# Gate and up projections of a SwiGLU block: more K-pairs in the seven-product form

## The chip, the core and the metric

The kernel runs on one core of a Trainium2 chip. TensorE (PE) multiplies, VectorE (DVE) and ScalarE (ACT) prepare operands and read results, SyncE (SP) issues the weight loads, GpSimd (POOL) has a little work at the start. The metric is the device time of one execution in microseconds (us), shown as the median of three runs. Besides these runs there is one profiled execution; its rows are what is read below.

## The reference, cut to what matters

One decoder layer on 256 tokens of width 2048: a mixer (not touched here), and then the SwiGLU block, followed by a final norm:

```
def swiglu(h, w_gate, w_up, w_down):
    return (jax.nn.silu(h @ w_gate) * (h @ w_up)) @ w_down

h = h + swiglu(rms_norm(h, norm_ffn[l]), w_gate[l], w_up[l], w_down[l])
```

`w_gate` and `w_up` are 2048 x 5632, `w_down` is 5632 x 2048, all float32. Every product is made from float32 operands that are cut into a high part (rounded to the multiplier's format) and a low part (the rest), as three matmuls: high x high, low x high, high x low.

## The kernel before

**Chunks and parts.** The 5632 hidden columns are cut into 11 chunks of 512 (`f` = 0 to 10). For a chunk the 512 gate columns and the 512 up columns are computed together. `PARTS` (L34) groups the chunks: 0 to 2, 3 to 5, 6 to 8, 9 to 10. After the chunks of a part come the products with their rows of `w_down` ("down"), four groups of 512 output columns. In a part of three the words first, middle and last chunk are used below.

**Pairs, units, forms.** The 2048 rows of a chunk's weights are 16 K-tiles, taken as eight pairs p = 0 to 7. A pair is a product of 2x2 blocks: two token tiles by two K-tiles, and two K-tiles by gate and up. In the eight-product form (kind "N") a pair is one unit of 8 block products, 24 matmuls of 512 columns. In the seven-product form (kind "W", Winograd's) it is two units: "Wp" with 3 block products (9 matmuls) and "Ws" with 4 (12 matmuls). Below, N3, P4 and S4 mean the N unit of pair 3 and the Wp and Ws units of pair 4; with a prime (N0', P2') they belong to the next chunk. `FFN_KINDS` (L35) gives the kinds of the eight pairs, the same for all chunks: units N0 N1 P2 S2 N3 P4 S4 N5 P6 S6 N7. The table `PRODUCTS` (L390) names for each product the PSUM bank it is added to: seven banks, numbered 1 to 7, hold a chunk's sums. There are eight banks in all (L63).

**Cutting a unit's weights (L422 to L437).** For an N unit ACT writes the high parts of the 4 blocks (L108, 128x2048) and DVE subtracts for the low parts (L109, 128x2048). For a Wp unit DVE first makes four sums of weight blocks (L433 to L435), then ACT and DVE cut 3 blocks (128x1536). The Ws unit cuts the four sums (128x2048); ACT can start only after L435.

**The tokens' side.** `Halves` keeps the tokens' high and low parts; `differences` (L150 to L169) adds what a pair's form needs: two difference blocks for N, four for W, high and low, in tiles of 16 blocks from the pool `late`, which holds three. With five N and three W pairs the 44 blocks fill three tiles. `fill` (L177) makes one pair from a transposed PSUM bank: two ACT copies, a split, then `differences`.

**Ends of a chunk.** After the last Ws unit of a chunk `squares_early` (L459, L460) reads three of the seven banks; after the last unit `squares_end` (L467 to L471) reads the other four. Then ACT applies SiLU (L944), DVE multiplies (L947, twice), and PE transposes the result in two halves (L954, four transposes each; called T0 and T1 here), each into a bank of its own, which is split into high and low by ACT and DVE (L956). This is a side chain of steps, of which one is taken after a unit: `squares_end` and SiLU after the first unit of the following chunk, the L947 after the second, T0 after the third, T1 after the fourth (for the last chunk of a part each one unit earlier).

**What sets the order.** The program is written out in order; each engine takes its instructions in that order and waits for semaphores. `run` (L486 to L547) decides it: before unit j is multiplied, units ahead of it are cut, up to four, as long as the `need` of the units from j on (2 for N, 3 for Wp, 2 for Ws) is at most `cap` = 9. Then unit j is multiplied, then at most one side step is taken. Weights, cuts, sums and activations share the pool `slots` of 22 buffers (L61); a new tile waits until the last reader of the buffer's former tile is done.

Of the kernel before, what the change touches and what calls it, by code (L numbers as in the profile page):

```python
# [11 lines left out]
F32R = mybir.dt.float32r  # L12
# [4 lines left out]
P = 128  # L17
# [14 lines left out]
KT = D_MODEL // P  # L32
CH = 512
PARTS = ((0, 3), (3, 6), (6, 9), (9, 11))  # L34
FFN_KINDS = "NNWNWNWN"  # L35
GATE_KINDS = "NWNWNWWN"


# [13 lines left out]
def trunk(ctx: ExitStack, tc: tile.TileContext, x, norm_mix, norm_ffn, w_in, w_pool, pool_scale,  # L52
# [19 lines left out]
    def name(s):  # L72
        uid[0] += 1
        return f"{s}_{uid[0]}"

    def slot(shape, dt=F32):
        return slots.tile([P] + shape, dt, tag="slot", name=name("slot"))

    def late_slot(shape, dt=F32):
        return late[0].tile([P] + shape, dt, tag="late", name=name("late"))  # L80
# [6 lines left out]
    def wk(dt=F32):  # L87
        return work.tile([P, CH], dt, tag="wk", name=name("wk"), bufs=8)
# [4 lines left out]
    def bank():  # L93
        return psum.tile([P, CH], F32, tag="bank", name=name("bank"))
# [4 lines left out]
    def cols(n):  # L99
        return slice(n * CH, (n + 1) * CH)  # L100

    def toks(t):
        return slice(t * P, (t + 1) * P)

    def split(hi, lo, src, scale=None):

        if scale is None:
            nc.scalar.activation(hi, src, AF.Copy)  # L108
            nc.vector.tensor_tensor(lo, src, f32(hi), OP.subtract)  # L109
        else:  # L110
            nc.scalar.activation(hi, src, AF.Copy, scale=scale)
            nc.vector.scalar_tensor_tensor(lo, src, scale, f32(hi), OP.mult, OP.subtract)
# [4 lines left out]
    class Lazily(dict):  # L117


        def __init__(self, make):  # L120
            self.make = make
# [5 lines left out]
    class Halves:  # L127
# [10 lines left out]
        def pair(self, p):  # L138

            part, k = self.parts[p // 2], p % 2 * 2  # L140
            return part[:, k:k + 2, 0, :], part[:, k:k + 2, 1, :]

        def slab(self, p, s):

            if isinstance(s, tuple):
                return [o[:, toks(s[1])] for o in self(2 * p + s[0])]
            tile, at, n = self.ext[p]
            return tile[:, at + s, :], tile[:, at + n + s, :]

        def differences(self, p, a):  # L150

            e = wk().rearrange("p (n s) -> p n s", s=P)
            n = 4 if self.kinds[p] == "W" else 2
            if n == 2:
                nc.vector.tensor_tensor(e[:, 0:2], a[:, :, 0], a[:, :, 1], OP.subtract)
            else:
                f = a.rearrange("p k t s -> p (k t) s")
                nc.vector.tensor_tensor(e[:, 0:2], f[:, 1:2].to_broadcast([P, 2, P]), f[:, 0:4:3], OP.subtract)
                nc.vector.tensor_tensor(e[:, 2], f[:, 0], e[:, 1], OP.subtract)
                nc.vector.tensor_tensor(e[:, 3], f[:, 2], e[:, 2], OP.subtract)  # L160
            for i, (tile, used) in enumerate(self.tiles):
                if used + 2 * n <= 16:
                    break
            else:
                i, tile, used = len(self.tiles), late_slot([16, P], F32R), 0
                self.tiles.append(None)
            self.tiles[i] = tile, used + 2 * n
            self.ext[p] = tile, used, n
            split(tile[:, used:used + n], tile[:, used + n:used + 2 * n], e[:, 0:n])  # L169

        def add_differences(self, p):
# [93 lines left out]
    def beside(gen, after=2, lag=2):  # L265
        side.append([clock[0] + after, lag, gen])
# [129 lines left out]
    class Squares:  # L396


        def __init__(self, lhs, load, after, early, before=None, kinds=FFN_KINDS):
            self.lhs, self.load, self.after, self.early, self.before = lhs, load, after, early, before  # L400
# [8 lines left out]
    class Square:  # L409
# [29 lines left out]
        def multiply(self):  # L439
            g = self.g  # L440
            wh, wl = self.w
            del self.w
            todo = PRODUCTS[self.kind]
            slab = [(b, *g.lhs().slab(self.p, s), k) for b, s, k in todo]
            steps = [(b, x, wh, k) for b, xh, xl, k in slab for x in (xh, xl)] + [(b, xh, wl, k) for b, xh, _, k in slab]
            for b, x, w, k in steps:
                start = b not in g.banks
                if start:
                    g.banks[b] = bank()
                g.left[b] -= 1  # L450
                nc.tensor.matmul(g.banks[b], x, w[:, k, :], start=start, stop=g.left[b] == 0)  # L451
            if self.ends:
                g.early(g.banks)

    def squares_early(b):

        c12, w, x = wk(), wk(), wk()
        nc.scalar.activation(c12, b[1], AF.Copy)
        nc.vector.tensor_tensor(w, b[6], c12, OP.subtract)  # L459
        nc.vector.tensor_tensor(x, b[7], w, OP.add)  # L460
        return c12, w, x
# [331 lines left out]
    mT, h, hT = [], [], []  # L793
# [131 lines left out]
    def load_gf():  # L925
        gf.append(slot([D_MODEL]))
        nc.sync.dma_start(gf[0], bass.AP(tensor=norm_final.tensor, offset=norm_final.offset,
                                         ap=[[0, P], [1, D_MODEL]]))

    def swiglu(f, last):  # L930

        early = []

        def load(raw, p):
            for i, w in enumerate((w_gate, w_up)):
                nc.sync.dma_start(raw[:, :, i, :], w[2 * p * P:2 * (p + 1) * P, cols(f)].rearrange("(j p) c -> p j c", p=P))

        def begin(b):
            early.append(squares_early(b))

        def finish(b):
            c = squares_end(b, early[0])
            for t in range(NT):
                nc.scalar.activation(c[t][0], c[t][0], AF.Silu, scale=rstd2[t])  # L944
            yield
            for t in range(NT):
                nc.vector.scalar_tensor_tensor(c[t][1], c[t][1], rstd2[t], c[t][0], OP.mult, OP.mult)  # L947
            yield
            act[f] = a = slot([8, SEQ], F32R)
            for k in range(2):  # L950
                pt = bank()
                for i in range(2):
                    for t in range(NT):
                        nc.tensor.transpose(pt[:, i * SEQ + t * P:i * SEQ + (t + 1) * P],  # L954
                                            c[t][1][:, (2 * k + i) * P:(2 * k + i + 1) * P], ident)
                split(a[:, 2 * k:2 * k + 2, :], a[:, 4 + 2 * k:6 + 2 * k, :], pair(pt))  # L956
                if k == 0:
                    yield
            ready.add(f)

        def before():
            cap[0] = 9

        def after(b):
            beside(finish(b), after=1 if last else 2, lag=1)

        return Squares(lambda: hT[0], load, after, begin, before)

    def down(part, n):
        f0, f1 = PARTS[part]  # L970
# [62 lines left out]
    for part, (f0, f1) in enumerate(PARTS):  # L1033
        for f in range(f0, f1):
            groups += [swiglu(f, f == f1 - 1)]
        k = 2 if f1 - f0 > 2 else 3
# [43 lines left out]
```

## Time and profile before

| | |
|---|---|
| time, median of 3 runs (lowest to highest) | 1556.91 us (1556.3 to 1557.02) |
| profiled execution, its own time | 1557.08 us |
| its span from first to last instruction | 1555.3 us |
| PE busy | 1543.5 us (99%) |
| DVE busy | 1093.0 us (70%) |
| ACT busy | 745.4 us (48%) |
| DMA | 192 GB/s over the span, queue q1 at 56.1% of 16 engines |

The span is 1.8 us shorter than the profiled execution's time; the rest lies around the span. Matmul ends are modelled, so the spacing of matmuls is better read from the chain of waits, where a piece has a start, a length and a count. A timeline row whose count is above 1 has merged instructions that follow each other; the bracket at its end is the idle time before it and what ended that.

### The profile page before, as it was taken

The page shows a single profiled execution, that of the slowest core. Times are in us where ns is not written, and L with a number is a line of the kernel's source. Part 1 is how long each engine was busy: PE and PEld are TensorE (multiplying, and loading weights), DVE is VectorE, ACT ScalarE, POOL GpSimd, SP SyncE. Part 2 cuts the span into 40 slices and gives each one's busy share as a digit, 9 for nine tenths or more (in the row PEclk, how much of TensorE's full clock was granted, in tenths as well). Part 3 has the DMA queues.
Part 4 walks back from the last instruction along what each step waited for, and adds up shares of the span by engine and source line. Part 5 has one row for each costly group of instructions (what it writes and reads, how often), then busy time and mean ns, then how long its engine had stood idle before and what let it go on. Part 6 is the DMA issues. An engine that isn't in the chain of part 4 may idle for free.

```text
span 1555.3 us, 19158 instructions
## 1 busy us (share of the span) xinstructions
PE 1543.5 (99%) x7895; PEld 1322.2 (85%) x7895; DVE 1093.0 (70%) x1056; ACT 745.4 (48%) x718; POOL 25.8 (2%) x94
## 2 busy tenths in 40 slices
PE   9999999999999999999999999999999999999997
PEld 9998999988888888888888788888888888888886
DVE  6453655644568898978656988666985769857685
ACT  7323343446555545546455555434554435544353
POOL 2000000101100000000000000000000000000000
PEclk9999999999999999999999999999999999999999
DMA  9654455554555746647554566555575555655651
GB/s 349 221 189 163 138 186 170 165 186 160 169 171 186 259 137 242 236 143 270 196 201 151 189 211 220 188 187 184 195 239 187 169 190 191 241 189 167 213 217 55
DMA packets 144456, 300.13 MB, mean 193 GB/s; under 512 B 6464, under 2 KB 8048, under 8 KB 144240
## 3 DMA queue, kind: packets, MB, share of 16 engines
q1 hardware_dynamic: 143600, 297.44, 56.1%
q8 instruction: 62, 1.02, 0.3%
q0 software_dynamic: 304, 1.06, 0.2%
q10 hardware_dynamic: 464, 0.40, 0.1%
q14 instruction: 26, 0.21, 0.0%
HBM read 296.77 MB, written 2.11 MB: 192 GB/s over the span
## 4 chain that ended last, share of the span: by engine, by line
PE 97%; DVE 1%; ACT 0%; issue 0%; DMA 0%; ACTq 0%; DVEq 0%
PE bank L451 38%; PE bank L344 14%; PE bank L345 14%; PE bank L349 14%; PE bank L364 5%; PE bank L372 5%; PE bank L366 5%; DVE slot L109 1%; PE bank L954 1%; PE bank L596 0%; DMA slot<-in_x_dram 0%; ACT slot L108 0%; PE bank L597 0%; PE bank L851 0%; PE bank L907 0%
## 5 line engine op out<-in xcount | busy, mean ns | idle before, releaser
L109 DVE TENSOR_TENSOR slot<-slot,slot 128x2048 fp32r<-128x2048 f32 (+3 forms) x406 | 718.9, 1798 | 185.5 <-ACT slot L108 184.9
L108 ACT ACTIVATE slot<-slot 128x2048 fp32r<-128x2048 f32 (+3 forms) x406 | 600.8, 1516 | 340.2 <-DVE slot L435 136.0
L451 PE MATMUL bank<-slot,slot 128*128 128x512 f32 x1719 | 439.2, 390 | 0.0
L451 PEld LDWEIGHTS bank<-slot,slot 128*128 128x128 f32 x1719 | 321.8, 188 | 66.5
L344 PE MATMUL bank<-slot,slot 128*128 128x512 f32 (+1 forms) x936 | 364.3, 390 | 0.0
L345 PE MATMUL bank<-slot,slot 128*128 128x512 f32 (+1 forms) x936 | 362.3, 388 | 0.0
L451 PE MATMUL bank<-slot,late 128*128 128x512 f32 x1014 | 279.3, 390 | 0.0
L349 PE MATMUL bank<-slot,slot 128*128 128x512 f32 (+1 forms) x936 | 236.5, 387 | 0.0
L451 PEld LDWEIGHTS bank<-slot,late 128*128 128x128 f32 x1014 | 189.7, 188 | 39.1
L344 PEld LDWEIGHTS bank<-slot,slot 128*128 128x128 f32 x936 | 175.9, 188 | 35.2
L345 PEld LDWEIGHTS bank<-slot,slot 128*128 128x128 f32 x936 | 175.9, 188 | 35.2
L349 PEld LDWEIGHTS bank<-slot,slot 128*128 128x128 f32 x936 | 174.9, 188 | 35.9
L364 PE MATMUL bank<-slot,slot 128*128 128x256 f32 x640 | 158.6, 286 | 0.0
L366 PE MATMUL bank<-slot,slot 128*128 128x256 f32 x640 | 156.9, 283 | 0.0
L366 PEld LDWEIGHTS bank<-slot,slot 128*128 128x128 f32 x640 | 122.8, 192 | 0.0
L364 PEld LDWEIGHTS bank<-slot,slot 128*128 128x128 f32 x640 | 122.7, 192 | 0.1
L372 PE MATMUL bank<-slot,slot 128*128 128x256 f32 x640 | 89.8, 283 | 0.0
L372 PEld LDWEIGHTS bank<-slot,slot 128*128 128x128 f32 x640 | 82.6, 192 | 0.0
L108 ACT ACTIVATE slot<-bank 128x512 fp32r<-128x512 f32 x38 | 22.6, 594 | 123.5 <-PE bank L954 67.8
L109 DVE TENSOR_TENSOR slot<-bank,slot 128x512 fp32r<-128x512 f32 x38 | 26.2, 689 | 54.0 <-ACT slot L108 54.0
L433 DVE TENSOR_TENSOR slot<-slot 128x1024 f32<-128x1024 f32 x49 | 59.6, 1217 | 0.0
L989 DVE TENSOR_TENSOR slot<-bank,slot 128x512 f32<-128x512 f32 x30 | 19.6, 685 | 55.5 <-PE bank L349 55.5
(162 smaller groups left out, 631.3 us busy)
## 6 DMA issues: line engine op xcount, KB each, us to landing
slot<-in_w_in_dram SPq DMA_DIRECT2D x103, 1024.0 KB, 5.0
slot<-in_w_gate_dram SPq DMA_DIRECT2D x88, 512.0 KB, 3.9
slot<-in_w_up_dram SPq DMA_DIRECT2D x88, 512.0 KB, 4.8
slot<-in_w_down_dram SPq DMA_DIRECT2D x44, 1024.0 KB, 5.1
slot<-in_w_out_dram SPq DMA_DIRECT2D x16, 1024.0 KB, 5.2
slot<-in_w_br_a_dram SPq DMA_DIRECT2D x8, 1024.0 KB, 5.0
slot<-in_w_br_b_dram SPq DMA_DIRECT2D x8, 1024.0 KB, 5.1
slot<-in_w_br_c_dram SPq DMA_DIRECT2D x8, 1024.0 KB, 5.0
```

Of the source, the lines that this page charges most:

```text
L108: nc.scalar.activation(hi, src, AF.Copy)
L109: nc.vector.tensor_tensor(lo, src, f32(hi), OP.subtract)
L344: nc.tensor.matmul(acc[:, c], hi[:, toks(t)], whi[:, j, c], start=i + j == 0, stop=False)
L345: nc.tensor.matmul(acc[:, c], lo[:, toks(t)], whi[:, j, c], start=False, stop=False)
L349: nc.tensor.matmul(acc[:, c], hi[:, toks(t)], wlo[:, j, c], start=False, stop=i + j == n - 1)
L364: nc.tensor.matmul(o, whi[:, j, w], hi, start=i + j == 0 and c % 2 == 0, stop=False, skip_group_check=True)
L366: nc.tensor.matmul(o, whi[:, j, w], lo, start=False, stop=False, skip_group_check=True)
L372: nc.tensor.matmul(o, wlo[:, j, w], hi, start=False, stop=i + j == n - 1 and c % 2 == 1, skip_group_check=True)
L433: nc.vector.tensor_tensor(s[:, 0:2], raw[:, 0:1].to_broadcast([P, 2, CH]), raw[:, 1:3], OP.add)
L451: nc.tensor.matmul(g.banks[b], x, w[:, k, :], start=start, stop=g.left[b] == 0)
L954: nc.tensor.transpose(pt[:, i * SEQ + t * P:i * SEQ + (t + 1) * P], c[t][1][:, (2 * k + i) * P:(2 * k + i + 1) * P], ident)
L989: nc.vector.tensor_add(h[t][:, cs], acc[t], h[t][:, cs])
```

## The change

`FFN_KINDS` gets a third letter, "B" at pair 1: both forms are prepared for it on the tokens' side, and each chunk picks one. The chunks in `inner` (1, 4 and 7, the middle chunks of the parts of three) take N as before; the other eight chunks take W, and their units are N0 P1 S1 P2 S2 N3 P4 S4 N5 P6 S6 N7. `slab`, `ext` and `differences` get the kind as a second key. The tokens' differences need 52 blocks instead of 44; where a fourth tile is opened, it comes from `slots` instead of `late`.

```
-FFN_KINDS = "NNWNWNWN"
+FFN_KINDS = "NBWNWNWN"
...
-        def slab(self, p, s):
+        def slab(self, p, kind, s):
...
-            tile, at, n = self.ext[p]
+            tile, at, n = self.ext[p, kind]
...
         def differences(self, p, a):
 
+            for kind in "WN" if self.kinds[p] == "B" else self.kinds[p]:
+                self.differences_of(kind, p, a)
+
+        def differences_of(self, kind, p, a):
             e = wk().rearrange("p (n s) -> p n s", s=P)
-            n = 4 if self.kinds[p] == "W" else 2
+            n = 4 if kind == "W" else 2
...
-                i, tile, used = len(self.tiles), late_slot([16, P], F32R), 0
+                i = len(self.tiles)
+                tile, used = (late_slot if i < 3 else slot)([16, P], F32R), 0
...
-            slab = [(b, *g.lhs().slab(self.p, s), k) for b, s, k in todo]
+            slab = [(b, *g.lhs().slab(self.p, self.kind[0], s), k) for b, s, k in todo]
...
+    inner = [f for f0, f1 in PARTS for f in range(f0 + 1, f1 - 1)]
...
-        return Squares(lambda: hT[0], load, after, begin, before)
+        return Squares(lambda: hT[0], load, after, begin, before, FFN_KINDS.replace("B", "N" if f in inner else "W"))
```

The built program has 2709 matmuls of the line L451 (L456 in the changed kernel) where there were 2733.

**VectorE at the start of a last chunk.** Before, at the start of chunk 5, from the first instruction of chunk 4's `squares_end`:

```order
L467 TENSOR_TENSOR wk_1104_8714<-bank_1067_8467,wk_1104_8714 128x512
L468 TENSOR_TENSOR wk_1116_8786<-bank_1067_8467,wk_1105_8715 128x512
L469 TENSOR_TENSOR wk_1104_8714<-bank_1068_8472,wk_1104_8714 128x512
L470 TENSOR_TENSOR wk_1103_8713<-bank_1065_8457,wk_1103_8713 128x512
L471 TENSOR_TENSOR wk_1105_8715<-bank_1066_8462,wk_1105_8715 128x512
L109 TENSOR_TENSOR slot_1118_8795<-slot_1099_8682,slot_1117_8794 128x2048
L947 SCALAR_TENSOR_TENSOR wk_1103_8713<-wk_1103_8713,st2_6_103,wk_1104_8714 128x512
L947 SCALAR_TENSOR_TENSOR wk_1105_8715<-wk_1105_8715,st2_6_103,wk_1116_8786 128x512
L109 TENSOR_TENSOR slot_1121_8837<-bank_1122_8838,slot_1121_8837 128x512
L433 TENSOR_TENSOR slot_1125_8847<-slot_1102_8698 128x1024
L434 TENSOR_TENSOR slot_1125_8847<-slot_1125_8847,slot_1102_8698 128x512
L435 TENSOR_TENSOR slot_1125_8847<-slot_1125_8847,slot_1102_8698 128x512
```

After the change the same place, from the fourth instruction of `squares_end` (L475 and L476 are L470 and L471 of before, L438 to L440 are L433 to L435, L954 is L947):

```order
L475 TENSOR_TENSOR wk_1114_8736<-bank_1076_8479,wk_1114_8736 128x512
L476 TENSOR_TENSOR wk_1116_8738<-bank_1077_8484,wk_1116_8738 128x512
L438 TENSOR_TENSOR slot_1127_8811<-slot_1107_8673 128x1024
L439 TENSOR_TENSOR slot_1127_8811<-slot_1127_8811,slot_1107_8673 128x512
L440 TENSOR_TENSOR slot_1127_8811<-slot_1127_8811,slot_1107_8673 128x512
L109 TENSOR_TENSOR slot_1126_8810<-slot_1107_8673,slot_1125_8809 128x1536
L954 SCALAR_TENSOR_TENSOR wk_1114_8736<-wk_1114_8736,st2_6_103,wk_1115_8737 128x512
L954 SCALAR_TENSOR_TENSOR wk_1116_8738<-wk_1116_8738,st2_6_103,wk_1124_8801 128x512
L109 TENSOR_TENSOR slot_1130_8830<-slot_1127_8811,slot_1129_8829 128x2048
L109 TENSOR_TENSOR slot_1133_8837<-slot_1110_8704,slot_1132_8836 128x2048
L109 TENSOR_TENSOR slot_1137_8857<-bank_1138_8858,slot_1137_8857 128x512
L109 TENSOR_TENSOR slot_1137_8857<-bank_1139_8874,slot_1137_8857 128x512
```

Before, N3 was cut ahead of the two multiplications, and the low part of the first transposed half (the 128x512 row that reads a bank) followed them at once. Now the cut of P2 stands ahead of them, and the cuts of S2 and N3 stand between them and that low part.

**TensorE at T1 of the same chunk.** Before:

```order
L451 MATMUL bank_1129_8862<-slot_1110_8752,late_763_6437 128x512
L451 MATMUL bank_1130_8865<-slot_1110_8752,late_763_6437 128x512
L451 MATMUL bank_1113_8763<-slot_1110_8752,slot_784_6564 128x512
L954 MATMUL bank_1131_8874<-ident_84,wk_1103_8713 128x128 [waits DVE_49]
L954 MATMUL bank_1131_8874<-ident_84,wk_1105_8715 128x128
L954 MATMUL bank_1131_8874<-ident_84,wk_1103_8713 128x128
L954 MATMUL bank_1131_8874<-ident_84,wk_1105_8715 128x128
L451 MATMUL bank_1112_8758<-slot_1117_8794,slot_784_6564 128x512 [waits Activation_49]
```

After the change (L961 is L954 of before):

```order
L456 MATMUL bank_1128_8817<-slot_1126_8810,slot_785_6570 128x512
L456 MATMUL bank_1120_8773<-slot_1126_8810,slot_785_6570 128x512
L456 MATMUL bank_1123_8788<-slot_1126_8810,late_787_6577 128x512
L961 MATMUL bank_1139_8874<-ident_84,wk_1114_8736 128x128 [waits DVE_49]
L961 MATMUL bank_1139_8874<-ident_84,wk_1116_8738 128x128
L961 MATMUL bank_1139_8874<-ident_84,wk_1114_8736 128x128
L961 MATMUL bank_1139_8874<-ident_84,wk_1116_8738 128x128
L456 MATMUL bank_1122_8783<-slot_1129_8829,late_787_6577 128x512 [waits Activation_49]
```

In both programs T1 takes the bank that T0 had, since the other seven hold the chunk's sums, and so it waits for the DVE instruction that reads T0's bank last. Before, T0 stood after P2 (57 matmuls into the chunk) and T1 after S2; now T0 stands after S1 (45 matmuls) and T1 after P2.

**VectorE at the start of the first chunk.** Before, from the low part of S2 in chunk 0 (128x2x256 rows are the splits of pairs 6 and 7 of the tokens, `late` rows their differences):

```order
L109 TENSOR_TENSOR slot_827_6855<-slot_823_6818,slot_826_6854 128x2048
L109 TENSOR_TENSOR slot_835_6897<-wk_834_6894,slot_835_6897 128x2x256
L158 TENSOR_TENSOR wk_836_6900<-wk_834_6894 128x256
L159 TENSOR_TENSOR wk_836_6900<-wk_834_6894,wk_836_6900 128x128
L160 TENSOR_TENSOR wk_836_6900<-wk_834_6894,wk_836_6900 128x128
L109 TENSOR_TENSOR late_837_6904<-wk_836_6900,late_837_6904 128x512
L109 TENSOR_TENSOR slot_839_6908<-slot_814_6744,slot_838_6907 128x2048
L109 TENSOR_TENSOR slot_835_6897<-wk_842_6943,slot_835_6897 128x2x256
L155 TENSOR_TENSOR wk_843_6948<-wk_842_6943 128x256
L109 TENSOR_TENSOR late_837_6904<-wk_843_6948,late_837_6904 128x256
```

After the change, from the differences of pair 6 on (its split stands ahead of these rows, right behind the two L918, which are L913 of before):

```order
L163 TENSOR_TENSOR wk_835_6900<-wk_833_6894,wk_835_6900 128x128
L164 TENSOR_TENSOR wk_835_6900<-wk_833_6894,wk_835_6900 128x128
L109 TENSOR_TENSOR late_813_6744<-wk_835_6900,late_813_6744 128x512
L438 TENSOR_TENSOR slot_838_6908<-slot_804_6696 128x1024
L439 TENSOR_TENSOR slot_838_6908<-slot_838_6908,slot_804_6696 128x512
L440 TENSOR_TENSOR slot_838_6908<-slot_838_6908,slot_804_6696 128x512
L109 TENSOR_TENSOR slot_837_6907<-slot_804_6696,slot_836_6906 128x1536
L109 TENSOR_TENSOR slot_834_6897<-wk_841_6929,slot_834_6897 128x2x256
L159 TENSOR_TENSOR wk_842_6934<-wk_841_6929 128x256
L109 TENSOR_TENSOR slot_843_6936<-wk_842_6934,slot_843_6936 128x256
L109 TENSOR_TENSOR slot_845_6940<-slot_838_6908,slot_844_6939 128x2048
L109 TENSOR_TENSOR slot_848_6947<-slot_816_6751,slot_847_6946 128x2048
```

P1 and S1 are now cut where N1 and P2 were, ahead of L913; P2 and S2, of which only S2 was left and stood ahead of pair 6, are cut behind it.

## Rows read from the trace of the kernel before

**Rows 1.** The page: span, two engines' busy time, and the shares of the chain of work that ended last.

```profile
span 1555.3 us, 19158 instructions
PE 1543.5 (99%) x7895; PEld 1322.2 (85%) x7895; DVE 1093.0 (70%) x1056; ACT 745.4 (48%) x718; POOL 25.8 (2%) x94
...
PE 97%; DVE 1%; ACT 0%; issue 0%; DMA 0%; ACTq 0%; DVEq 0%
```

**Rows 2.** The chain of waits in order of time (start, length, engine, tile, line, count), at the first chunk of all and in the part of chunks 3 to 5.

```profile
849.12 12.29 PE bank L451 x54
861.44 2.28 DVE slot L109
...
892.80 1.33 DVE wk L947 x2
894.73 2.76 PE bank L451 x12
...
1032.49 54.40 PE bank L451 x240
1087.33 2.76 PE bank L451 x12
1090.52 38.80 PE bank L451 x171
1129.76 2.78 PE bank L451 x12
```

**Rows 3.** Busy time of the engines in four stretches: the output projection ahead of chunk 0; the three chunks 3 to 5; around T0 of chunk 0's result; the end of the program. Columns: stretch, its length, busy us and (in brackets) instructions of PE, PEld, DVE, ACT and POOL, granted clock, DMA share, GB/s.

```profile
725.00:837.00 112.00, 112.00 (x515) 92.67 (x514) 71.52 (x69) 55.87 (x64) 0.00 (x0) 1.00 0.61 205
...
1032.50:1160.00 127.50, 127.50 (x571) 105.56 (x571) 107.44 (x86) 60.41 (x42) 0.00 (x0) 1.00 0.60 202
...
892.00:898.00 6.00, 4.82 (x25) 3.58 (x25) 4.64 (x6) 1.97 (x2) 0.00 (x0) 1.00 0.58 181
...
1550.00:1555.30 5.30, 0.00 (x0) 0.00 (x0) 0.00 (x0) 0.05 (x1) 0.00 (x0) 0.53 0.60 198
```

**Rows 4.** The timeline of DVE from the end of chunk 4's cuts to the first transposed half of its result (chunk 5 begins inside).

```profile
1103.04 8.90 DVE L109 TENSOR_TENSOR slot<-slot,slot 128x2048 fp32r<-128x2048 f32 x4 [0.38 <-ACT slot L108]
1111.86 0.68 DVE L459 TENSOR_TENSOR wk<-bank,wk 128x512 f32<-128x512 f32 x1
...
1113.18 1.22 DVE L433 TENSOR_TENSOR slot<-slot 128x1024 f32<-128x1024 f32 x1
...
1115.77 1.75 DVE L109 TENSOR_TENSOR slot<-slot,slot 128x1536 fp32r<-128x1536 f32 x1
1117.90 2.29 DVE L109 TENSOR_TENSOR slot<-slot,slot 128x2048 fp32r<-128x2048 f32 x1 [0.38 <-ACT slot L108]
1120.11 0.68 DVE L467 TENSOR_TENSOR wk<-bank,wk 128x512 f32<-128x512 f32 x1
...
1122.50 0.68 DVE L471 TENSOR_TENSOR wk<-bank,wk 128x512 f32<-128x512 f32 x1
1125.19 2.29 DVE L109 TENSOR_TENSOR slot<-slot,slot 128x2048 fp32r<-128x2048 f32 x1 [2.02 <-ACT slot L108]
1127.40 1.41 DVE L947 SCALAR_TENSOR_TENSOR wk<-wk,st,wk 128x512 f32<-128x512 f32 x2
1130.42 0.69 DVE L109 TENSOR_TENSOR slot<-bank,slot 128x512 fp32r<-128x512 f32 x1 [1.61 <-ACT slot L108]
```

**Rows 5.** The timeline of DVE in chunk 3: its start, its last cut, the early reading of its banks, and the low part of its first transposed half.

```profile
1032.30 1.29 DVE L989 TENSOR_TENSOR slot<-bank,slot 128x512 f32<-128x512 f32 x2 [6.19 <-PE bank L349]
...
1059.46 2.29 DVE L109 TENSOR_TENSOR slot<-slot,slot 128x2048 fp32r<-128x2048 f32 x1 [0.25 <-ACT slot L108]
1068.41 0.69 DVE L459 TENSOR_TENSOR wk<-bank,wk 128x512 f32<-128x512 f32 x1 [6.66 <-PE bank L451]
...
1088.06 0.69 DVE L109 TENSOR_TENSOR slot<-bank,slot 128x512 fp32r<-128x512 f32 x1 [2.74 <-ACT slot L108]
```

**Rows 6.** The timeline of DVE in chunk 0, from L913 to the two L947.

```profile
838.28 1.28 DVE L913 TENSOR_TENSOR slot<-bank,wk 128x512 f32<-128x512 f32 x2
842.17 2.29 DVE L109 TENSOR_TENSOR slot<-slot,slot 128x2048 fp32r<-128x2048 f32 x1 [2.61 <-ACT slot L108]
844.79 0.69 DVE L109 TENSOR_TENSOR slot<-wk,slot 128x512 fp32r<-128x512 f32 x1 [0.32 <-ACT slot L108]
...
848.98 2.29 DVE L109 TENSOR_TENSOR slot<-slot,slot 128x2048 fp32r<-128x2048 f32 x1 [1.12 <-ACT slot L108]
...
877.18 0.68 DVE L459 TENSOR_TENSOR wk<-bank,wk 128x512 f32<-128x512 f32 x1
...
892.72 1.41 DVE L947 SCALAR_TENSOR_TENSOR wk<-wk,st,wk 128x512 f32<-128x512 f32 x2
```

**Rows 7.** The timeline of ACT: the copies of pair 6 of the tokens, the high parts of S6, N7, N0' and N1' in chunk 4, and the high part of a transposed half.

```profile
843.25 0.85 ACT L182 ACTIVATE wk<-bank,ncols 128x256 f32<-128x256 f32 x2 [1.11 <-PE bank L907]
...
1101.09 7.33 ACT L108 ACTIVATE slot<-slot 128x2048 fp32r<-128x2048 f32 x4 [4.15 <-DVE slot L435]
...
1129.79 0.60 ACT L108 ACTIVATE slot<-bank 128x512 fp32r<-128x512 f32 x1 [4.63 <-PE bank L954]
```

**Rows 8.** The page's row for the loads of the up weights: count, size, median us from issue to landing.

```profile
slot<-in_w_up_dram SPq DMA_DIRECT2D x88, 512.0 KB, 4.8
```

**Rows 9.** The timeline of SP: the load of chunk 5's pair 1.

```profile
1097.39 0.37 SPq L936 DMA_DIRECT2D slot<-in_w_gate_dram  x1
```

More of the change, by code (lines that the diff above doesn't have):

```diff
@@ L164, in differences @@
             else:
-                i, tile, used = len(self.tiles), late_slot([16, P], F32R), 0
+                i = len(self.tiles)
+                tile, used = (late_slot if i < 3 else slot)([16, P], F32R), 0
                 self.tiles.append(None)
             self.tiles[i] = tile, used + 2 * n
-            self.ext[p] = tile, used, n
+            self.ext[p, kind] = tile, used, n
             split(tile[:, used:used + n], tile[:, used + n:used + 2 * n], e[:, 0:n])
```

## The prediction

> **What bounds the kernel now.** I read the page first: PE is busy for 99% of the span and holds 97% of the chain that ended last, DVE 70% and ACT 48% [rows 1]. The reader is to see there that time can only be won by taking work from PE, and that DVE is far from full as a mean. The chain in order of time comes next [rows 2]. In chunk 3 it runs through 240 matmuls in a row, 54.40 us, so 0.2267 us each, with no gap; between its pieces lie 0.44 us, the transposes. In chunk 0 it is different: from 861.44 to 894.13 the chain goes through DVE. The windows then give the means of stages [rows 3]: in chunks 3 to 5 DVE is busy for 107.4 of 127.5 us, 84%, well above the page's mean. What this hides, and where it stops hiding, is read from the timeline of DVE [rows 4 to 6].
>
> **Term 1, PE's work.** Eight chunks lose one eight-product pair and gain a seven-product one: 24 - 21 = 3 matmuls each, 24 in all, 24 x 0.2267 = 5.44 us, 0.68 us a chunk [rows 2].
>
> [...]
>
> **Term 2, DVE's work.** An N cut costs DVE 2.2 us (four from 1103.04 to 1111.86). A W pair costs 4.3 us for the sums and the P cut (1113.18 to the end at 1117.5) and 2.2 us for S, with 0.38 us of waiting for ACT between [rows 4]. So each of the eight chunks gives DVE 4.3 us more and PE 0.68 us less. It comes down to where DVE is late for PE, which is at T0 and T1 of the preceding chunk's result.
>
> **First chunks 3, 6 and 9.** Read at chunk 3 [rows 5]. P1 and S1 are cut ahead of the two L989, in DVE's idle 6.19 us. Behind them the remaining cuts ran from 1033.5 to 1061.7; P2 joins them, +4.3, so 1066.0. DVE then waited 6.66 us, until 1068.4, for PE to reach L459; PE now gets there 0.68 us sooner, at 1067.7. That leaves 1.7 us. Nothing is lost: -0.68 us each, -2.0 us. That DVE is early there also shows behind it: the low part of the first transposed half, at 1088.06, had waited 2.74 us for T0. If that cover were gone, each further us of DVE would move T0 by as much.
>
> **Last chunks 2, 5 and 8.** Read at chunk 5 [rows 2, 4]. It begins on PE at 1116.40: T0 at 1090.52 + 38.80 = 1129.32, less 57 x 0.2267. T0 is now due after 45 matmuls, at 1126.60, and T1 after the transposes' 0.44 and P2's 9 x 0.2267, at 1129.08. DVE: the fourth N cut began at 1109.65. In its place stands P1, to 1113.95; the early reading takes 1.32 (1111.86 to 1113.18), to 1115.27; S1, 1117.5; `squares_end`, 3.0 (1120.11 to 1123.1), 1120.5; P2, 1124.8; the L947, 1.4, 1126.2. T0 is in time by 0.4 us. But T1 needs T0's bank, whose last reader is the low part of the first half, 0.6 us; in the new order the cuts of S2 and N3 stand ahead of it. 1126.2 + 2 x 2.2 + 0.6 = 1131.2, where 1129.08 was due: PE waits 2.1 us. ACT's half of the split (0.60 us after the transposes [rows 7]) is ready long before. Before the change T1 was not held up, since that low part followed the L947 and T0 at once.
>
> Behind T1, DVE has two W pairs, two N cuts and two for the down products ahead of L459, 2 x 6.9 + 4 x 2.2 = 22.6, and the second half's low part, 0.6: about 1154.8 after T1's transposes. PE has 102 matmuls there, 23.1 us, to the same 1154.8. No second wait, then. Each of these chunks: -0.68 + 2.1 = +1.4 us, +4.3 us for three. The trace of before has no such wait, so its bounds: 0, if the low part finds DVE free; 4.3 us, with one more 2.2 us cut between. I take 2.1, since each duration in it has its own row.
>
> **Chunk 10** follows a first chunk, in which DVE waits for PE ahead of L459, so it starts from there. With chunk 3's rows [rows 2, 5]: 1068.41 + 1.32 + 2.2 is 1071.9, `squares_end` must wait for the chunk's end on PE at 1073.97 and lasts to 1077.0; P2, the L947, S2, N3 and the low part add 4.3 + 1.4 + 4.4 + 0.6, 1087.7. T1 is due 12.68 us after the chunk's start, 1086.65. PE waits 1.05 us: +0.4 us net.
>
> **Chunk 0.** Here DVE is on the path already [rows 2, 6]: the L947 end at 894.13, T0 follows, and PE idles 1.2 us around it [rows 3]. Pair 6 of the tokens is split at 844.79; it can't come sooner, since ACT's copies wait for PE's transposes until 843.25 [rows 7]. Before, S2 was cut at 842.17, in that wait. Now S2 and the whole of P2 are cut behind pair 6: 4.3 + 2.2 = 6.5 us more between 844.79 and the L947, a stretch with little idle time. One wait of 1.12 us ahead of N3 goes, since P2 fills it; S2 now waits for ACT, which makes the high part of pair 7's differences first, about as long. T0 moves from 894.2 to 900.7, and all behind it: +6.5 us, in which chunk 0's own 0.68 us is lost. Bounds: 3.4 us if that 1.12 and 2 us more of waits are filled, 7.9 with S2's wait on top. I take 6.5, what the row durations give.
>
> **Edits costed at nothing.** Pair 1's second set of differences (about 1.7 us of DVE) lies in the output projection, where DVE is busy for 71.5 of 112 us [rows 3]; the other way, 1.7 us once. The fourth tile of differences takes one of 22 slots to the end: the loads hide it (below, with its price).
>
> **Sum.** +6.5 + 4.3 - 2.0 + 0.4 = +9.2 us. Against the profiled execution's 1557.08 us (span 1555.3 and 1.8 around it) that is 1566.3; the median lies 0.17 lower: 1566.1 us.
>
> **Rivals.**
> *All is hidden.* -5.44: 1551.6 us. For it: PE's 97% of the chain and the 240 without a gap. Against: DVE holds the chain in chunk 0, and the order puts 4.4 us of cuts between T0 and T1.
> *Only chunk 0 loses.* The T1 waits vanish if the low part runs sooner: +6.5 - 7 x 0.68 = +1.7, 1558.8 us. Against: DVE goes strictly by its order.
> *Only the T1 waits.* Chunk 0's addition disappears in waits for ACT: -5.44 + 3 x 2.1 + 1.05 = +1.9, 1559.0 us. Against: the idle time in the stretch is a few us in all.
> *Slower still, by the lost slot.* A load would be issued a unit later. Chunk 5's pair 1 is issued at 1097.39 [rows 9], first read by ACT's fourth high part, 1101.09 + 3 x 1.83 = 1106.6 [rows 7], 9.2 us later; landing takes 4.8 [rows 8]. It decides from 4.4 us of delay; a whole unit's 5.44 would leave 1.0 us of waiting, in 11 chunks 11 us: 1577 us. For it: the pool has no spare. Against: that load now waits for the matmuls of P4 in chunk 4, about 1098, nearly where it stood.
> [...]
> That the change does not remove matmuls is out: the built program has 24 fewer.
>
> **How the numbers follow.** Forecast 0.72, all hidden 0.05, only chunk 0 0.07, only T1 0.07, lost slot 0.06, clock 0.03. What a measurement can tell from no change is 0.2%, 3.1 us: 1553.8 to 1560.0. Faster: 0.05. Within: 0.14, the two half cases. Slower: 0.81. The likeliest case alone goes from 1563 to 1569; with the half cases the range is 1558.5 to 1570.
>
> **What would show it.** In the changed profile: 2709 matmuls of the product line at 0.227 us; in the chain, DVE up to T0 of chunk 0's result near 900.7; at T1 in chunks 2, 5 and 8 an idle time of PE's transposes near 2 us whose releaser is L109 on DVE, about 1 us in chunk 10, and none in chunks 3, 6, 9 and in the middle ones. [...] No wait in any place makes the prediction wrong as a whole.

## The result, and the profile after

The changed kernel takes 1569.74 us (median of 4 runs, 1567.49 to 1570.66), the kernel before 1556.73 us (1556.3 to 1557.02): +13.0 us, a ratio of 1.0082 with an interval of 1.0066 to 1.0098. Slower, as forecast, and within the range; the forecast 1566.1 lies 3.6 us below. It is a narrow hit: two of the four runs, 1570.55 and 1570.66 us, lie above the range's end of 1570.

The chain of waits of the kernel after, in order of time, at the places of [rows 2]: the first matmuls of chunks 0, 3, 6 and 9, and what follows T1 in chunks 2, 5, 8 and 10, for chunk 8 with T1 itself (start, length, engine, tile, line, count).

```profile
836.68 5.45 PE bank L456 x24
...
945.19 30.21 PE bank L456 x126
...
1041.66 53.72 PE bank L456 x237
...
1140.35 30.20 PE bank L456 x126
...
1236.81 53.72 PE bank L456 x237
...
1334.84 1.08 PE bank L961 x4
1335.92 29.77 PE bank L456 x126
...
1431.94 40.36 PE bank L456 x178
...
1486.70 28.60 PE bank L456 x126
```

The same places in the kernel before; 1032.49 is in [rows 2].

```profile
837.33 5.44 PE bank L451 x24
...
1225.09 54.40 PE bank L451 x240
...
1417.69 54.40 PE bank L451 x240
```

Differences of the starts are the lengths of the four parts, each with its down projection. Before: 195.16, 192.60, 192.60, and 137.6 to the end of the span at 1555.3. After: 204.98, 195.15, 195.13, and 137.06 to 1569.0. So +9.82, +2.55, +2.53 and -0.55; with a start 0.65 earlier that is the whole 13.7 us by which the span grew. The second thing to see is the length of equal work: 126 matmuls behind T1 take 28.60 us in chunk 10, 0.227 each, but 30.21, 30.20 and 29.77 in chunks 2, 5 and 8. In chunk 8 T1 is slow as well, 1.08 us for its four transposes where chunk 2's take 0.66 (below), so each of the three places loses 1.6 us.

The view of what PE waited for, in the kernel after (total, times, longest, us):

```profile
PE bank L961 <- DVE slot L109: 6.7, 4, 2.1
PE bank L456 <- ACT slot L108: 2.2, 1, 2.2
PE bank L456 <- DVE slot L109: 1.9, 1, 1.9
...
PE bank L961 <- DVE wk L954: 0.7, 2, 0.4
```

The first line is T1: four waits, and DVE's low part as releaser. The next two are in chunk 0: at 854.70 us the first matmul of S2 waits for its high part from ACT (2.2 us), and at 851.51 P2 waits for its low part from DVE (1.9 us). In the kernel before, T0 of chunk 0's result waited 1.2 us in all [rows 3], and nothing else here.

The timeline of DVE around T1 in chunk 2, kernel after; it answers to [rows 4]:

```profile
936.40 1.75 DVE L109 TENSOR_TENSOR slot<-slot,slot 128x1536 fp32r<-128x1536 f32 x1
938.07 1.41 DVE L954 SCALAR_TENSOR_TENSOR wk<-wk,st,wk 128x512 f32<-128x512 f32 x2
939.39 4.49 DVE L109 TENSOR_TENSOR slot<-slot,slot 128x2048 fp32r<-128x2048 f32 x2
943.80 0.68 DVE L109 TENSOR_TENSOR slot<-bank,slot 128x512 fp32r<-128x512 f32 x1
```

And PE there: T0, the last matmul of P2, and T1:

```profile
939.89 0.60 PE L961 MATMUL bank<-ident,wk 128*128 128x128 f32 x4
...
942.17 0.39 PE L456 MATMUL bank<-slot,late 128*128 128x512 f32 x1
944.54 0.66 PE L961 MATMUL bank<-ident,wk 128*128 128x128 f32 x4 [1.98 <-DVE slot L109]
```

T0 is in time by 0.4 us: the two L954 end at 939.48, and PE reaches it at 939.89. The cuts of S2 and N3 (939.39, two in 4.49 us) stand between L954 and the low part of T0's half, which ends at 944.48; T1, which needs that bank, starts at 944.54. This is the order that the prediction read, and the 5.0 us from 939.48 to 944.48 are its 4.4 and 0.6. One more thing is to be read here: the 1.98 us count from the end of the matmul before, 942.17 + 0.39. Where matmuls follow one another they do so every 0.227 us, so T1 could have begun at 942.40, and 2.14 us are lost. So a wait of PE costs about 0.16 us more here than the view says.

Busy time in stretches of the kernel after (columns as in [rows 3]): chunk 0, behind T1 in chunks 2, 5 and 8, and around T1 in chunk 10.

```profile
853.00:861.00 8.00, 6.30 (x16) 4.94 (x17) 6.18 (x11) 4.94 (x5) 0.00 (x0) 0.57 0.40 131
...
945.00:950.00 5.00, 5.00 (x17) 3.96 (x16) 4.07 (x5) 2.81 (x3) 0.00 (x0) 0.66 0.60 208
...
1140.00:1145.00 5.00, 5.00 (x19) 3.95 (x17) 3.91 (x5) 2.58 (x3) 0.00 (x0) 0.66 0.63 210
...
1335.00:1340.00 5.00, 5.00 (x18) 4.13 (x18) 3.34 (x5) 2.02 (x3) 0.00 (x0) 0.67 0.63 210
...
1480.00:1490.00 10.00, 9.41 (x46) 7.51 (x46) 8.55 (x9) 4.38 (x5) 0.00 (x0) 1.00 0.67 213
```

The number to read is the granted clock, third from the right. Behind T1 of chunk 2 it is 0.90, 0.50, 0.50, 0.50 and 0.89 in the five single us from 945 to 950, and 1.00 before and after them. Read as two levels, 1.00 and 0.50, the mean of 0.66 over 5 us is 3.4 us at the lower one. Five matmuls from 946.91 to 949.04 come every 0.43 us there, in place of 0.227. By that 3.4 us lose 1.6 us of work, as much as the chain shows. Such a stretch is called a fall below. One stands behind each of the three T1 waits of 2 us and one in chunk 0, none at chunk 10's wait of 0.59 us. This is what the sum of the prediction lacks.

### The profile page after: what moved, and what is told of

Its sections match the earlier page's. It is cut to its first block, busy times and chain, and to the rows that moved or that the text cites. A ratio compares the mean times of both kernels' runs of the same rounds, so it can differ in the third digit from the quotient of the medians.

```text
span 1569.0 us, 19183 instructions
## 1 busy us (share of the span) xinstructions
PE 1547.0 (99%) x7871; PEld 1322.4 (84%) x7871; DVE 1127.7 (72%) x1092; ACT 758.6 (48%) x727; POOL 25.8 (2%) x94
## 4 chain that ended last, share of the span: by engine, by line
PE 88%; DVE 8%; issue 2%; ACT 1%; ACTq 0%; DVEq 0%; POOL 0%; POOLq 0%
PE bank L456 29%; PE bank L349 13%; PE bank L350 13%; PE bank L354 13%; PE bank L369 5%; PE bank L377 5%; PE bank L371 5%; DVE slot L109 4%; ACT slot L108 1%; DVE slot L438 1%; DVE slot L439 1%; DVE slot L440 1%; PE bank L961 1%; PE bank L601 0%; DVE wk L954 0%
## 5 line engine op out<-in xcount | busy, mean ns | idle before, releaser
L109 DVE TENSOR_TENSOR slot<-slot,slot 128x2048 fp32r<-128x2048 f32 (+3 forms) x414 | 732.4, 1797 | 182.5 <-ACT slot L108 182.4
L108 ACT ACTIVATE slot<-slot 128x2048 fp32r<-128x2048 f32 (+3 forms) x414 | 612.2, 1515 | 347.0 <-DVE slot L440 161.7
L456 PE MATMUL bank<-slot,slot 128*128 128x512 f32 x1713 | 438.5, 391 | 2.0 <-DVE slot L109 1.9
L456 PEld LDWEIGHTS bank<-slot,slot 128*128 128x128 f32 x1713 | 322.4, 189 | 70.0 <-DVE slot L109 2.4
L456 PE MATMUL bank<-slot,late 128*128 128x512 f32 x996 | 279.1, 397 | 2.2 <-ACT slot L108 2.2
L456 PEld LDWEIGHTS bank<-slot,late 128*128 128x128 f32 x996 | 189.6, 191 | 42.2 <-ACT slot L108 2.7
L438 DVE TENSOR_TENSOR slot<-slot 128x1024 f32<-128x1024 f32 x57 | 69.3, 1216 | 0.1
```

What stands on the lines that cost most here:

```text
L438: nc.vector.tensor_tensor(s[:, 0:2], raw[:, 0:1].to_broadcast([P, 2, CH]), raw[:, 1:3], OP.add)
```

## The experiments

The theory after this profile has three parts: DVE's order at T1, DVE's path in chunk 0, and a clock that falls behind the waits. The rivals: the slot taken from the pool; DVE too full wherever the work is put; a clock that falls by itself.

**Where the loss is: one place at a time.** Three kernels take four W pairs in some chunks only, a fourth in none, with the second set of differences kept.

```diff
-    inner = [f for f0, f1 in PARTS for f in range(f0 + 1, f1 - 1)]
+    inner = [f for f in range(11) if f not in (3, 6, 9)]      # first chunks
+    inner = [f for f in range(11) if f not in (2, 5, 8, 10)]  # last chunks and chunk 10
+    inner = [f for f in range(11) if f not in (0,)]           # chunk 0
+    inner = list(range(11))                                   # none
```

> Four W pairs only in the first chunks 3, 6 and 9; the other eight chunks as before, the extra set of differences and its slot as after. Theory (DVE's order at T1, chunk 0's DVE path, and a clock that falls behind the waits): first chunks are free, 9 matmuls less, -2.0 us, about 1554.7, no wait of PE beyond before's, granted clock 0.998. Rival 'lost slot': the slot is missing here too, so most of the 13 us stay, above 1565. Rival 'DVE is full, wherever the work is put': three eighths of the 13 us, about 1561.6.

Measured: 1554.73 us (before, run beside it, 1556.6), ratio 0.9988 (0.9979 to 0.9997): -1.9 us, and no wait in these chunks. First chunks are free.

> Four W pairs only in chunks 2, 5, 8 and 10. Theory: 12 matmuls less, -2.7; T1 waits 2.1, 2.1, 2.1 and 1.05, +7.4; the clock at its lower level for some 3 us behind each of the three longer waits, 1.5 us lost each, +4.5: in all +9.2, about 1565.9, clock near 0.995. Without the fall of the clock +4.6, 1561.3. Rival 'DVE is full anywhere': half of the 13 us, 1563.2, and not at these four places alone.

Measured: 1563.29 us (1562.17 to 1565.18), 1.0044 (1.0029 to 1.0059). PE's transposes T1 of chunks 2 and 5 in this kernel:

```profile
937.99 0.65 PE L961 MATMUL bank<-ident,wk 128*128 128x128 f32 x4 [1.97 <-DVE slot L109]
...
1133.80 0.66 PE L961 MATMUL bank<-ident,wk 128*128 128x128 f32 x4 [2.09 <-DVE slot L109]
```

The stretches behind them:

```profile
938.00:943.00 5.00, 5.00 (x17) 4.10 (x18) 3.62 (x5) 2.35 (x3) 0.00 (x0) 0.66 0.63 210
...
1132.00:1137.00 5.00, 3.20 (x16) 2.73 (x17) 3.58 (x5) 1.98 (x2) 0.00 (x0) 1.00 0.55 177
```

The waits are those of the changed kernel, but the clock fell behind the first alone; three falls had been expected. Without a fall the second part is 1.6 us longer than before (1035.07 to 1229.30, 194.2 us), with one the first is 3.1 longer. So a wait of 2 us may or may not bring a fall; one costs some 1.5 us.

> Four W pairs only in chunk 0. Theory: DVE sets the end of chunk 0, T0 comes 6 to 6.7 us later against the chunk's start, and the half-rate stretch at 854 to 860.5 us lies in the time that PE would spend waiting for DVE at T0 anyway, so +6.5, about 1563.2. If the half-rate stretch adds to it: +9.5, 1566.2. Rival 'lost slot' as in the run with the first chunks: above 1565, with waits in the later chunks, which this theory leaves as before.

Measured: 1563.4 us (1563.01 to 1563.96), +6.8. T0's followers start at 901.29, 64.12 us after the chunk, in place of 57.40 [rows 2]. The lower level lasted here for about 3.4 us (0.76 over 854 to 861), and in the run of the whole change with T1 later, below, for 6.9 (0.51), yet there the followers also start 64.12 us after the chunk. What the longer stretch costs comes off PE's wait at T0, 1.9 us here and 0.8 there. So the lower level costs nothing in chunk 0, since PE waits for DVE at T0 either way. That DVE's added cuts make the 6.7 us can be read in the changed kernel: from pair 6's split to the L954 (844.14 to 898.77) it takes 54.63 us and is busy for 48.17, before (844.79 to 892.72) 47.93 and 41.78. Its idle time hardly changed, since the wait for ACT ahead of N3 went and one ahead of S2 came:

```profile
854.68 4.49 DVE L109 TENSOR_TENSOR slot<-slot,slot 128x2048 fp32r<-128x2048 f32 x2 [1.38 <-ACT slot L108]
```

No run moves these cuts by themselves.

> The second set of differences of pair 1 is made and keeps its slot, but every chunk takes pair 1 in eight products, as before: the same matmuls as before. Theory: the slot costs nothing and the differences lie in the output projection: 1556.7 within 0.8. Rival 'lost slot': a load comes a unit late in many chunks, 1560 to 1568.

Measured: 1556.5 us, 0.9998 (0.9989 to 1.0007). The slot and the second set cost nothing; the rival is out. The three changes alone sum to -1.9 + 6.7 + 6.8 = +11.6, the whole to +13.0. The rest goes with the number of falls: one in the profile of the last chunks alone, three behind T1 in that of the whole.

**Order or load?** Chunk 0 is left as before and T1 is put one unit later.

```diff
-    inner = [f for f0, f1 in PARTS for f in range(f0 + 1, f1 - 1)]
+    inner = [0] + [f for f0, f1 in PARTS for f in range(f0 + 1, f1 - 1)]
...
                 if k == 0:
-                    yield
+                    yield 2 if f in (1, 4, 7, 9) else 1
```

> The change without chunk 0, and T1 issued one unit later (behind S2 rather than P2) in chunks 2, 5, 8 and 10. Theory: T1 was late by 2.1 us and S2's 12 matmuls are 2.72 us, so PE finds the bank free, no wait, and with no wait no fall of the clock: 21 matmuls less, -4.8 us, 1551.8, clock 0.998. Rival 'DVE is full there': the wait comes back at a cut behind T1 in the same chunks, 1557 to 1562. Rival 'the clock falls by the work, not by the wait': clock near 0.996 still.

Measured: 1551.55 us (1551.36 to 1552.17), ratio 0.9966 (0.9953 to 0.9979): faster than before by 5.3 us, though DVE is busy for 1122.8 us, 29.8 more than before. What PE waited for:

```profile
PE bank L222 <- POOL ident masks.py:199: 1.4, 1, 1.4
PE bank L961 <- DVE wk L954: 1.2, 2, 0.8
```

Only lines that the kernel before has too are left, and there is no fall (mean clock 0.999). In all, six of the profiles have no wait above 1.2 us inside the chunks (before, first chunks, no chunk, T1 later, and two further below); none of the six has a fall there (mean clocks 0.998 and 0.999, where the profile of the last chunks alone, with one fall, has 0.997), which speaks against a clock that falls by itself. The whole change with T1 later, chunk 0 too (the second edit alone):

> The whole change, chunk 0 too, with nothing but T1 one unit later in chunks 2, 5, 8 and 10. Theory: the four waits and the falls of the clock behind them go, chunk 0's 6.7 us stay: 1551.55 + 6.8 (what chunk 0 alone added) = 1558.3, the only stretch at the lower level in chunk 0. Rival 'the falls come from the work of the whole stretch': some of the 4.5 us of falls stay, above 1560.

Measured: 1558.22 us (1558.04 to 1558.82, 10 runs). T1's place is thus worth 11.5 of the 13.0 us: four waits and three falls; chunk 0 is worth 6.7; and the work removed gives the rest back.

**The fourth W pair at another pair.** Chunk 0 keeps its units of before.

```diff
-FFN_KINDS = "NBWNWNWN"
+FFN_KINDS = "NNWNWBWN"
```

> The change without chunk 0, and with the fourth W pair at pair 5 in place of pair 1, T1 where it was. Theory (DVE's strict order): around T0 and T1 all is as before, so no wait there, but W pairs 4, 5 and 6 now follow one another at 6.9 us of DVE against 4.76 of PE: in chunks 2, 5, 8 and 10 the cuts of P6 and S6 come about 2.6 us late, +1.9 net each, while chunks 3, 6 and 9 stay at -0.68: about 1562, PE's waits at the product line and not at the transposes. Rival 'the wait belongs to T1's bank alone': no wait at all, 1551.8.

Measured: 1564.13 us (1563.35 to 1565.22). The waits are at another place than expected:

```profile
PE bank L961 <- DVE wk L954: 6.1, 10, 2.2
PE bank L456 <- DVE slot L109: 2.6, 5, 0.6
```

The product line waits 0.6 us a time, not 2.6; the rest of DVE's lateness comes to PE at the next T0, in the down projection. T1 doesn't wait. That DVE's order decides is borne out, its place was misread. Set against the parts of before less the matmuls removed, the four parts are 4.4, 2.4, 2.4 and 2.4 us longer, so each of the chunks 2, 5, 8 and 10 lost 2.4 us, where 2.6 had been expected. The other 2.0 us are in chunk 0: with pair 5's second set of differences its cuts come later, T0 of its result waits 2.55 us (2.21 and 0.34) in place of 1.2, and what follows T0 starts 59.4 us after the chunk in place of 57.4. The waits listed, 8.7 - 1.2 = 7.5 us, don't make up for the loss of 11.6 us. The weight loads' own view of the same kernel lists more waits, among them short ones that end before the matmul ahead has:

```profile
PEld bank L961 <- DVE wk L954: 9.1, 10, 2.6
PEld bank L456 <- DVE slot L109: 6.2, 10, 1.1
```

Ten at the product line where the view of PE shows five. The loss lies between the two views (7.5, and 15.3 less the 1.8 that the kernel with T1 later shows). This profile has no fall, though its longest wait is 2.21 us: its mean clock is 0.998, and the 12 matmuls behind that wait take 2.78 us, as in the kernel before (2.76 [rows 2]).

**The wait by itself, in doses, in the kernel before.**

```diff
+                if k == 0:
+                    for _ in range({1: 9, 4: 11, 7: 14, 9: 9}.get(f, 0)):
+                        nc.vector.tensor_tensor(c[0][0], c[0][0], c[1][0], OP.subtract)
                 split(a[:, 2 * k:2 * k + 2, :], a[:, 4 + 2 * k:6 + 2 * k, :], pair(pt))
```

> The kernel before, with 9, 11, 14 and 9 extra subtractions of 128x512 (0.60 us of DVE each, their result is not used) ahead of the low part of T0's half in chunks 2, 5, 8 and 10. By the rows of before 1.6 us of DVE idle time (2.7 in chunk 10) and 1.3 us of T1's slack hide the first part: waits of T1 of 2.5, 3.7, 5.5 and 1.4 us, 13.1 in all, and the matmuls are as many as before. Theory (the clock falls behind some waits of 2 us and more, and not behind 1 us): 1556.6 + 13.1 + 1.6 for each fall, three falls: about 1574.5, with stretches at the lower level of 3.2 us behind chunks 2, 5 and 8. Rival 'no fall from a wait alone': 1569.7, clock 0.998. Rival 'the longer the wait, the longer the lower level': stretches growing from 2.5 to 5.5 us of waiting.

Measured: 1580.7 us (1579.94 to 1582.96), profiled 1580.01. T1's waits were 3.37, 4.81, 7.00 and 2.30 us, 17.5 in all, 0.9 to 1.5 more each than worked out, since a subtraction took 0.71 us of DVE (nine from 936.13 to 942.54) and not 0.60. The stretches, in chunks 2, 5, 8 and 10:

```profile
944.00:948.00 4.00, 4.00 (x12) 3.12 (x11) 3.62 (x5) 2.15 (x2) 0.00 (x0) 0.57 0.09 32
1142.00:1146.00 4.00, 3.50 (x11) 2.98 (x12) 3.93 (x5) 0.94 (x1) 0.00 (x0) 0.57 0.05 18
1340.00:1348.00 8.00, 4.19 (x14) 3.54 (x15) 7.79 (x10) 1.63 (x1) 0.00 (x0) 0.57 0.15 59
1498.00:1504.00 6.00, 6.00 (x29) 5.02 (x30) 5.61 (x5) 3.46 (x3) 0.00 (x0) 1.00 0.00 0
```

So a wait alone, with the matmuls of before, can bring a fall. Three fell, behind 3.37, 4.81 and 7.00 us; the 2.30 us did not. The first two stretches are alike, 3.4 us; the longest wait has 6.9 us, about half of it within the wait itself. The span grew by 22.9 us against the kernel before: 17.5 of waits, four times 0.16, and 4.6 for the falls (1.6, 1.5 and 1.5 in T1 and the 114 matmuls behind it) make 22.7.

**How much room has DVE?** All from the kernel with T1 later. A fifth W pair, at pair 3, in chunks 3, 6 and 9:

```diff
-FFN_KINDS = "NBWNWNWN"
+FFN_KINDS = "NBWCWNWN"
...
+            for kind in "WN" if self.kinds[p] in "BC" else self.kinds[p]:
...
+        return Squares(lambda: hT[0], load, after, begin, before, FFN_KINDS.replace("C", "W" if f in (3, 6, 9) else "N").replace("B", "N" if f in inner else "W"))
```

> The run with T1 later, and a fifth W pair (pair 3) in chunks 3, 6 and 9. In chunk 3 DVE waited 2.31 us for PE ahead of the early reading, so there is room for 2.3 of the 4.3 us. Theory: the cut of N0 of the next chunk and the early reading come 2.9 us later against PE's 0.68 sooner, T0 in the chunk behind waits 1.2 to 2.1 us: between +0.5 and +1.4 net each, 1553 to 1556, and falls of the clock only if waits pass 2 us. Rival 'first chunks have room for more': -0.68 each, 1549.5.

Measured: 1557.72 us (1556.3 to 1558.11). That is above the 1553 to 1556 expected. In chunks 4, 7 and 10 T0 waits 1.17 us (0.83 and 0.34), and parts two to four grow by 0.9 to 1.0 us each, as expected. The other 3.8 us of the profile lie in the first part: pair 3's second set of differences moves chunk 0's cuts, T0 of its result waits 2.55 us, and a fall follows it (the 12 matmuls behind T0 take 4.34 us). That was a side effect of the edit. The same wait stood in the run with pair 5, without a fall (first that run, then this one):

```profile
895.05 0.33 PE L961 MATMUL bank<-ident,wk 128*128 128x128 f32 x1 [2.21 <-DVE wk L954]
...
895.03 0.33 PE L961 MATMUL bank<-ident,wk 128*128 128x128 f32 x1 [2.21 <-DVE wk L954]
```

Even within this kernel it varies: four of the ten runs took 1556.3 to 1556.8 us at a mean clock of 0.998, the others 1557.7 to 1558.1 at 0.997.

Four W pairs in the middle chunks too, with T1 one unit later there as well:

```diff
-    inner = [0] + [f for f0, f1 in PARTS for f in range(f0 + 1, f1 - 1)]
+    inner = [0]
...
-                    yield 2 if f in (1, 4, 7, 9) else 1
+                    yield 2 if f != 2 and f != 5 and f != 8 and f != 10 else 1
```

> The run with T1 later, and four W pairs in the middle chunks 1, 4 and 7 too, T1 later there as well. Theory (DVE has no idle time left there): T0 had 0.4 us to spare in chunks 2, 5 and 8; with 4.3 us more of DVE and 0.68 less of PE it waits 4.5 us, +3.9 net each: about 1563, more with falls of the clock behind these waits (1.6 each, up to 1568). Rival 'with T1 later there is room': -0.68 each, 1549.5.

Measured: 1549.93 us (1549.89 to 1550.73), ratio 0.9958 (0.9944 to 0.9971). My theory fell; the rival's 1549.5 came. DVE in chunks 3 and 4 with T1 later alone (middle chunk with three W pairs), where it waits:

```profile
1066.34 0.69 DVE L464 TENSOR_TENSOR wk<-bank,wk 128x512 f32<-128x512 f32 x1 [2.31 <-PE bank L456]
...
1079.68 2.29 DVE L109 TENSOR_TENSOR slot<-slot,slot 128x2048 fp32r<-128x2048 f32 x1 [2.02 <-ACT slot L108]
1081.89 1.41 DVE L954 SCALAR_TENSOR_TENSOR wk<-wk,st,wk 128x512 f32<-128x512 f32 x2
1085.98 0.69 DVE L109 TENSOR_TENSOR slot<-bank,slot 128x512 fp32r<-128x512 f32 x1 [2.68 <-ACT slot L108]
```

And with four W pairs in the middle chunk:

```profile
1066.90 0.69 DVE L464 TENSOR_TENSOR wk<-bank,wk 128x512 f32<-128x512 f32 x1 [0.26 <-PE bank L456]
...
1072.04 0.69 DVE L472 TENSOR_TENSOR wk<-bank,wk 128x512 f32<-128x512 f32 x1 [1.53 <-PE bank L456]
...
1079.29 1.41 DVE L954 SCALAR_TENSOR_TENSOR wk<-wk,st,wk 128x512 f32<-128x512 f32 x2
1080.62 4.49 DVE L109 TENSOR_TENSOR slot<-slot,slot 128x2048 fp32r<-128x2048 f32 x2
1085.02 0.68 DVE L109 TENSOR_TENSOR slot<-bank,slot 128x512 fp32r<-128x512 f32 x1
```

The four-W order keeps DVE from waiting: 2.31 + 2.02 + 2.68 = 7.0 us of idle time here become 0.26 + 1.53 = 1.8. The 5.2 us hold P1's 4.3. The two cuts in front of the low part, which made T1 late, stand in what had been DVE's wait for T0.

Pair 4 of chunk 0 in eight products:

```diff
-FFN_KINDS = "NBWNWNWN"
+FFN_KINDS = "NBWNDNWN"
...
+            for kind in "WN" if self.kinds[p] in "BD" else self.kinds[p]:
...
+        return Squares(lambda: hT[0], load, after, begin, before, FFN_KINDS.replace("D", "W" if f else "N").replace("B", "N" if f in inner else "W"))
```

> The run with T1 later, and pair 4 of chunk 0 in eight products, so that chunk 0 has two W pairs. Theory (chunk 0 is bound by DVE behind pair 6): 4.3 us of DVE go there, PE's 1.2 us of waiting at T0 vanish, 3 matmuls more cost 0.68: -0.5, 1551.0. Rival 'chunk 0 is bound by something else': +0.7, 1552.2.

Measured: 1552.06 us (1551.94 to 1552.46), +0.5, against the theory. DVE's waits for ACT in this kernel, ahead of cuts that W's sums had filled:

```profile
855.23 2.29 DVE L109 TENSOR_TENSOR slot<-slot,slot 128x2048 fp32r<-128x2048 f32 x1 [1.38 <-ACT slot L108]
...
861.30 2.29 DVE L109 TENSOR_TENSOR slot<-slot,slot 128x2048 fp32r<-128x2048 f32 x1 [2.26 <-ACT slot L108]
```

The same lesson from the other side: DVE's work went, its idle time came.

From the fastest version, T0 of chunk 0's result one unit later:

```diff
                 nc.vector.scalar_tensor_tensor(c[t][1], c[t][1], rstd2[t], c[t][0], OP.mult, OP.mult)
-            yield
+            yield 1 if f else 2
```

> The run with four W pairs everywhere but in chunk 0, and T0 of chunk 0's result one unit later (behind P2 of chunk 1 rather than S1). Theory (PE waits 1.2 us there only because the multiplication with the other half, L954, ends late, and P2's 9 matmuls, 2.0 us, can go ahead): the wait goes, 1549.93 - 1.2 = 1548.7. Rival 'DVE takes the wait further': it comes back at a cut of chunk 1, 1549.9.

Measured: 1551.7 us (1550.38 to 1552.68), 1.8 us slower than without the edit. PE's T0 in chunk 2:

```profile
932.54 0.33 PE L961 MATMUL bank<-ident,wk 128*128 128x128 f32 x1 [1.52 <-DVE wk L954]
933.20 0.55 PE L961 MATMUL bank<-ident,wk 128*128 128x128 f32 x3 [0.33 <-DVE wk L954]
```

The wait left chunk 1 and came back here, as the rival said, and behind it the clock fell (0.50 from 934 to 937), after 1.85 us of waiting in two pieces, where chunk 1's T0 had waited 1.2. Three of the six runs have a mean clock of 0.997 and take 1552.1 to 1552.7 us, the others 0.998 and 1550.4 to 1551.3.

## Why the prediction was right, and what it lacked

- *PE's work* held: the page has 1713 matmuls of the product line with the tokens' operand in a `slot` tile and 996 with it in a `late` tile, 2709 in all; 237 in a row in 53.72 us, 0.2267 each.
- *First chunks* held: -2.0 forecast, -1.9 with them alone.
- *Last chunks*: the wait of 2.1 us was right to 0.1 us, in place, releaser and size. The net +1.4 measured 1.6 without a fall (parts two and three of the run with the last chunks alone), and 3.2 with one. No second wait followed behind T1, as forecast.
- *Chunk 10*: 1.05 us of wait forecast, 0.59 measured; part four is 0.55 us shorter, forecast 0.3.
- *Chunk 0*: +6.5 forecast, +6.7 measured in the distance from the chunk's start to T0's followers, +6.8 alone. The reason held too: DVE is busy 6.4 us longer behind pair 6, and S2 waits 1.38 us for ACT where N3 had waited 1.12. That PE would wait for P2 and S2 on the way was not forecast, and costs nothing.
- *Slot and second set at nothing* held.
- *The step that failed* is the clock. That it falls behind the waits has a chance of 0.03 and no term in the sum: the 1.00 around a wait of 1.2 us in two pieces [rows 3] was taken as evidence for waits of 2.1 us in one. By parts the forecast says +7.9, +0.7, +0.7 and -0.3, the profile +9.82, +2.55, +2.53 and -0.55. The missing 1.8 to 1.9 us in each of the first three is a fall of 1.6 us and the 0.16 that a wait costs beyond the view. The three falls, 4.9 us, are nearly all of what lies between the sum of +9.2 and the parts' +14.35; the rest, 0.5 of waits beyond the view, 0.2 in chunk 0 and 0.3 less in chunk 10, nearly cancels. A start 0.65 us earlier, which no term has, brings the 14.35 to 13.7. The lower level lasted about 3.4 us each time at T1 (0.66, 0.66 and 0.67 over 5 us), behind three of its four waits.
- *Luck*: the range was made for half cases and small errors of the waits, not for falls. The median came out inside it by 0.3 us. The profiled run, with a fall behind each of the three waits, lies above it at 1570.66 us; the two runs inside it have higher mean clocks (0.994 and 0.996 against 0.993).
- *Right with a thinner reason than it looked*: the prediction priced DVE's added work at T1 in that order, and was right; the same way of adding, used on the middle chunks with T1 later, was wrong by 13 us (about 1563 expected, 1549.93 measured).

## What to carry to other kernels

When an edit makes the units of a hand-ordered pipeline shorter, look at what is placed by count of units: here PE's second transpose came one unit too early for its bank, and one unit later turned +13.0 us into +1.4, and without chunk 0 into -5.3. An engine's idle time belongs to an order: before pricing added work at an engine that waits, see whether the new order still has that wait. Price a single PE wait of about 2 us with a possible fall of the clock on top, here 1.5 to 1.6 us.

## What the runs showed of the hardware

- The lower level of TensorE's clock (0.50 granted) behind a short wait: in the profiles a fall came behind T1 waits of 1.97 to 2.09 us (four times of six), 3.37, 4.81 and 7.00 us, behind waits at T0 of 1.85 us and, in one of two kernels, 2.55 us (each in two pieces), and in chunk 0 with its two waits of 1.9 and 2.2 us. None came behind 0.59, 1.2 and 2.30. In T1 and the matmuls behind it a fall cost 1.5 to 1.6 us, after waits of 1.97 us and of 7.00 us alike. What decides at about 2 us is open, and wasn't tried further: nearly the same wait in chunk 5 brought a fall in one kernel (2.08 us) and none in another (2.09 us).
- Versions with such waits scatter: 1567.49 to 1570.66 and 1562.17 to 1565.18 us, mean clock 0.996 to 0.993 and 0.998 to 0.996, the longest with the lowest (the changed kernel and the one with the last chunks alone); the version with T1 later and chunk 0 as before, which has no such wait, kept 0.8 us.
- The fastest version, four W pairs in all chunks but the first with T1 later, is at 1549.93 us, 0.42% below the kernel before.
